# A build-time scheduler that reserves the shared SBUF port of VectorE and GpSimd, with new priorities, in a two-layer attention and RG-LRU block

## The chip, the cores and the metric

The kernel runs on one core of one Trainium2 chip, in one launch. The metric is the device time of that launch in microseconds (us). The engines are named as the profile names them: PE (TensorE matmul) and PEld (its weight load), DVE (VectorE), ACT (ScalarE), POOL (GpSimd), SP (SyncE, which issues most DMAs).

## What is computed

One sequence of 1024 latent tokens `x` and 256 context tokens `ctx`, width 1024, passes through two layers. Layer 0 is windowed grouped-query attention (16 heads, 4 key/value heads, 128-token blocks, all context keys in the same softmax, a sink logit per head), layer 1 is a bidirectional RG-LRU. A squared-ReLU MLP of width 4096 follows each. Only the latent stream is returned.

```python
for i in range(DEPTH):                       # DEPTH = 2
    mx = split(silu(c) @ ada_w[i] + ada_b[i], 6); mc = split(silu(c_ctx) @ ada_w[i] + ada_b[i], 6)
    h_x = modulate(rms_norm(x, g[0]), mx[0], mx[1]); h_c = modulate(rms_norm(ctx, g[0]), mc[0], mc[1])
    y_x, y_c = attention_mixer(...) if i % 2 == 0 else rglru_mixer(...)
    x = x + mx[2] * rms_norm(y_x, g[1])
    x = x + mx[5] * rms_norm(sqrelu_mlp(modulate(rms_norm(x, g[2]), mx[3], mx[4]), w1[i], w2[i]), g[3])
    # the same for ctx, in layer 0 only
...
# rglru_coeffs (d = direction), then a scan h = a * h + bx over the tokens
r = sigmoid(u @ w_a[d] + b_a[d]); i = sigmoid(u @ w_i[d] + b_i[d])
log_a = -8 * softplus(-lam[d]) * r
a, bx = exp(log_a), sqrt(-expm1(2 * log_a)) * (i * u)
...
y_x = (gelu(h_x @ w_gate) * (rec_forward + rec_backward)) @ w_out
```

## The kernel before, in words

Tokens lie in 8 latent and 2 context tiles of 128. Each fp32 operand of a matmul is split into a high part, its value rounded to fp32r by a cast (line 254, on ACT or DVE), and a low part, the value minus the high part (a tensor_tensor with two SBUF inputs, on DVE or GpSimd). A product is three matmuls: lines 259, 260 and 261. So the stream of matmuls is fed by casts on ACT or DVE and subtractions on DVE or GpSimd. Those subtractions stand in line 638 for the attention weights (`w`), line 679 for the first layer's normed inputs (`h`), lines 1658 and 1909 for later ones, line 1590 for the output projection's weights, line 2220 for its inputs `z`.

Nothing in the program text fixes the order of the work. A class `Plan` (lines 43 to 183) takes every operation with the engine or engines that may do it, a duration in ns, a priority (`key`), its dependences and its buffers (`add`, `any`). `order` then plays the plan through at build time: it starts the operation that can start earliest, among those within `eps` of it on the same engine the one of lowest key; where an operation may go to a second engine, it goes there only if it would end there no later than on the first one plus `alt`. `emit` writes each engine's instructions in that order, and on the chip each engine runs its own list in order and waits for semaphores.

There are four plans, played one after the other: `project` (keys `KEYS0`: norms, the modulation rows, weight splits, q, k and v, rope), the attention (`KEYS`), one for MLP 0 and everything up to and including layer 1's recurrence, output projection and residual (`KEYS2`), and MLP 1 (`KEYS3`). In a plan with `cal` set, the durations go through the line `CAL`. It is set in `KEYS2` alone (from the last part of MLP 0 on), and there `order` also knows of the port that DVE and GpSimd share: an operation in the set `two` (one that may go to either engine, or is marked) takes up to 0.43 of its length longer on DVE if it starts while GpSimd works on one.

The lines that the change and the prediction speak of:
- line 589 (`row`): a modulation row, DVE multiplies a 128x1024 tile of weights `raw` by the SiLU vector `srow` and sums it; 57 of them in `project`. Line 593 (`row_pool`): the same product on GpSimd, with the sum on ACT (line 596), for those context rows whose entry in the tables `cp` and `cq` is 1: 23 of 40. Line 1249: rows of the same kind later on.
- line 805: the low part of `q` (`qd`), line 572: the scaling `xn` by the norm (on GpSimd, ACT or DVE).
- layer 1's recurrence: lines 2112, 2116, 2120 and 2144 make gates and inputs of the scans, line 2152 is the scan (on a 128x1024 tile forward, two of 512 backward, 256 for context), lines 2185 and 2188 add the two directions and multiply by the gate, line 2220 splits the result.
- line 1746: `y<-y,py`, DVE adds a PSUM tile of the output projection to `y`; PE waits for it where it needs the PSUM tile again.
- lines 1690 to 1720: norm and residual between sub-layers (`part`, `root`, the product with `G` in line 1704, `x` in line 1706).

Of the kernel before, what the change touches and what calls it, by code (L numbers as in the profile page):

```python
# [42 lines left out]
class Plan:  # L43
    ENG = {"PE": mybir.EngineType.PE, "ACT": mybir.EngineType.Activation, "DVE": mybir.EngineType.DVE, "Pool": mybir.EngineType.Pool}
    CAL = {"PE": (1.045, 0), "ACT": (1, 105), "DVE": (1.077, 35), "Pool": (1.24, -56)}
    LAT = {"PE": 230, "ACT": 140, "DVE": 135, "Pool": 150, "DMA": 100, "Q": 900}

    def __init__(self, slots, keys, start={}):
        self.keys = keys
        self.start = start  # L50
# [35 lines left out]
    def order(self):  # L86
# [2192 lines left out]
```

## Time and profile before

| | |
|---|---|
| median of 3 runs | 2811.51 us (2810.71 to 2811.72) |
| the profiled execution's own time | 2807.43 us |
| its span, first to last instruction | 2805.7 us |
| granted TensorE clock, mean | 0.978 |
| PE busy | 2654.4 us, 95%, 12886 instructions |
| PEld busy | 2194.4 us, 78% |
| DVE busy | 2072.5 us, 74%, 3088 instructions |
| ACT busy | 1130.3 us, 40%, 2105 instructions |
| POOL busy | 899.1 us, 32%, 767 instructions |
| DMA | 392.23 MB, mean 140 GB/s |

How to read it: the profile is one execution. Its own time is 4.1 us under the median of the runs, and 1.7 us above its span. Busy shares are means over stages of very different make-up, so the windows view further down, which gives busy time by stretch, tells more than this table. The stretches used there are: 0 to 239 us (`project`), 239 to 660 (the rest of the projections, attention), 660 to 805 (attention's end, start of MLP 0), 805 to 1480 (MLP 0), 1480 to 1800 (its end, residual, start of layer 1), 1800 to 2080 (recurrence and output projection), 2080 to 2185 (residual, start of MLP 1), 2185 to 2780 (MLP 1).

### The profile page before, as it was taken

What the parts mean: (1) busy time and instruction counts of PE and PEld (TensorE: products, weight loads), DVE (VectorE), ACT (ScalarE), POOL (GpSimd) and SP (SyncE); (2) the same over time, 40 slices, a digit from 0 to 9 for tenths busy, and PEclk for the clock granted to TensorE, in tenths of its full rate; (3) what the DMA queues carried; (4) which work ended last, traced back from release to release, by engine and by line L of the source; (5) the groups of instructions that cost most, each with busy time, mean ns of one, the idle gap of its engine ahead of it and who ended that gap; (6) DMA issues with size and microseconds to landing.
All of it is one profiled execution on the core that took longest, in us unless ns stands there. A gap on an engine that the chain in (4) does not pass through costs nothing.

```text
span 2805.7 us, 35386 instructions
## 1 busy us (share of the span) xinstructions
PE 2654.4 (95%) x12886; PEld 2194.4 (78%) x12886; DVE 2072.5 (74%) x3088; ACT 1130.3 (40%) x2105; POOL 899.1 (32%) x767
## 2 busy tenths in 40 slices
PE   6798999998999999999999999989888999999997
PEld 4677788877788888888888888877666888888886
DVE  8988999997777776766657667699699776654546
ACT  5325777776322223211115434777535222221101
POOL 7653344444411103221116211254258211111113
PEclk9899999999999999999999999999999999999999
DMA  6462321214255556655554235654242333333323
GB/s 235 154 224 87 117 76 46 69 46 173 79 183 176 182 191 199 191 186 167 191 164 156 81 105 202 209 213 170 71 156 78 112 120 110 132 125 98 116 75 125
DMA packets 132613, 392.23 MB, mean 140 GB/s; under 512 B 14756, under 2 KB 17748, under 8 KB 128600
## 3 DMA queue, kind: packets, MB, share of 16 engines
q1 hardware_dynamic: 128984, 377.40, 39.9%
q10 hardware_dynamic: 3456, 12.58, 1.1%
q8 instruction: 101, 1.65, 0.3%
q14 instruction: 72, 0.59, 0.1%
HBM read 280.58 MB, written 109.35 MB: 139 GB/s over the span
## 4 chain that ended last, share of the span: by engine, by line
PE 68%; DVE 13%; POOL 4%; ACT 4%; issue 3%; DMA 2%; SPq 0%; DVEq 0%; ACTq 0%; POOLq 0%
PE pf L261 10%; PE pf L259 10%; PE pf L260 10%; PE py L260 9%; PE py L261 9%; PE py L259 9%; PE py L1103 2%; PE tp L1020 1%; DVE x L1706 1%; PE pv L1034 1%; DVE sc L990 1%; PE pg L260 1%; PE pg L259 1%; PE pg L261 1%; DVE gi L2152 1%
## 5 line engine op out<-in xcount | busy, mean ns | idle before, releaser
L260 PE MATMUL pf<-h,w 128*128 128x512 f32 (+1 forms) x1400 | 511.3, 365 | 5.9 <-POOL h L1658 5.6
L261 PE MATMUL pf<-h,w 128*128 128x512 f32 (+1 forms) x1400 | 511.3, 365 | 4.1 <-DVE w L1444 3.1
L259 PE MATMUL pf<-h,w 128*128 128x512 f32 (+1 forms) x1400 | 512.0, 366 | 1.6 <-ACT hf L1653 1.6
L1565 DVE TENSOR_TENSOR y<-y,py 128x512 f32<-128x512 f32 x268 | 183.0, 685 | 272.6 <-PE py L261 272.6
L260 PEld LDWEIGHTS pf<-h,w 128*128 128x128 f32 x1400 | 265.1, 189 | 48.6 <-POOL h L1658 6.8
L261 PEld LDWEIGHTS pf<-h,w 128*128 128x128 f32 x1400 | 264.8, 189 | 48.1 <-DVE w L1444 3.9
L259 PEld LDWEIGHTS pf<-h,w 128*128 128x128 f32 x1400 | 265.1, 189 | 44.7 <-ACT hf L1653 2.0
L1538 POOL TENSOR_TENSOR hw<-raw,hw 128x512 fp32r<-128x512 f32 x78 | 109.4, 1408 | 580.5 <-DVE hw L254 306.7
L254 ACT CAST w<-raw 128x1024 fp32r<-128x1024 f32 x126 | 131.9, 1049 | 320.0 <-PE pf L261 107.5
L259 PE MATMUL py<-hw,hw 128*128 128x512 f32 x592 | 230.4, 389 | 0.0
L261 PE MATMUL py<-hw,hw 128*128 128x512 f32 x592 | 230.3, 389 | 0.0
L260 PE MATMUL py<-hw,hw 128*128 128x512 f32 x592 | 230.3, 389 | 0.0
L254 ACT CAST hw<-raw 128x512 fp32r<-128x512 f32 x113 | 68.7, 621 | 387.5 <-DMA raw<-in_w 166.0
L1014 POOL TENSOR_SCALAR P<-P,sc 128x640 f32<-128x640 f32 (+2 forms) x160 | 118.3, 752 | 180.0 <-DVE sc L1011 94.3
L259 PE MATMUL py<-w,hw 128*128 128x512 f32 x432 | 168.2, 389 | 0.0
L261 PE MATMUL py<-w,hw 128*128 128x512 f32 x432 | 168.1, 389 | 0.0
L260 PE MATMUL py<-w,hw 128*128 128x512 f32 x432 | 168.1, 389 | 0.0
L1103 PE MATMUL py<-w,oT 128*128 128x512 f32 x480 | 146.5, 409 | 2.8 <-DVE w L938 2.1
L997 ACT ACTIVATE P<-S,sc 128x640 f32<-128x640 f32 (+2 forms) x160 | 113.9, 712 | 52.8 <-DVE sc L991 35.4
L259 PEld LDWEIGHTS py<-hw,hw 128*128 128x128 f32 x592 | 111.1, 188 | 23.2
L260 PEld LDWEIGHTS py<-hw,hw 128*128 128x128 f32 x592 | 111.1, 188 | 23.1
L261 PEld LDWEIGHTS py<-hw,hw 128*128 128x128 f32 x592 | 111.1, 188 | 23.0
(298 smaller groups left out, 6405.4 us busy)
## 6 DMA issues: line engine op xcount, KB each, us to landing
raw<-in_w SPq DMA_DIRECT2D x128, 512.0 KB, 3.8
raw<-in_ada_t SPq DMA_DIRECT2D x96, 512.0 KB, 4.6
raw<-hid_d SPq DMA_DIRECT2D x64, 512.0 KB, 4.5
w<-ws_d SPq DMA_DIRECT2D x30, 1024.0 KB, 6.2
hid_d<-c SPq DMA_DIRECT2D x112, 256.0 KB, 2.3
ws_d<-pw SPq DMA_DIRECT2D x80, 256.0 KB, 2.9
x<-x_d SPq DMA_DIRECT2D x26, 512.0 KB, 4.5
x_d<-x SPq DMA_DIRECT2D x24, 512.0 KB, 2.6
```

The lines of the kernel that those rows point to most:

```text
L254: (e.copy if e is self.nc.scalar else e.tensor_copy)(out=out, in_=x)
L259: mm(o, lhsT=lh, rhs=rh, start=start, stop=False, skip_group_check=on)
L260: mm(o, lhsT=lh, rhs=rl, start=False, stop=False, skip_group_check=on)
L261: mm(o, lhsT=ll, rhs=rh, start=False, stop=stop, skip_group_check=on)
L990: nc.vector.tensor_reduce(out=nmx[:, j:j + 1], in_=z["S", j][:, 256:256 + n], op=ALU.max, axis=AX.X, negate=True)
L997: nc.scalar.activation(out=z["P"][j][:, :n], in_=z["S", j][:, 256:256 + n], func=AF.Exp, scale=0.125, bias=negm[:, j:j + 1], accum_out=l[: ...
L1014: nc.gpsimd.tensor_scalar(out=z["P"][j][:, :n], in0=z["P"][j][:, :n], scalar1=z["sc"][3][:, j:j + 1], scalar2=1.0, op0=ALU.mult, op1=ALU.mult)
L1020: nc.tensor.transpose(z["tp", i][:, j * P:(j + 1) * P], z["P"][j][:, i * P:(i + 1) * P], self.ident)
L1034: mm(z["acc"], lhsT=v, rhs=z["pt", i][:, e], start=i + e == 0, stop=e == 1 and i == len(keys) - 1)
L1103: nc.tensor.matmul(z["ps", n], lhsT=oT[k // 2][2]["oT"][:, x, k % 2], rhs=Wo[k][:, w, n * 512:(n + 1) * 512], start=m == 0, stop=m == 3 * ...
L1538: e.tensor_tensor(out=z[n][:, 1], in0=z["raw"][:, s], in1=z[n][:, 0].bitcast(F32), op=ALU.subtract)
L1565: nc.vector.tensor_tensor(out=y, in0=y, in1=z["ps"], op=ALU.add)
```

## The change

The planner treats the port as something that one engine holds at a time. Each operation names the engines on which it holds the port (`two`, a string: "DVE", "Pool", "DVE Pool" or empty). `order` keeps until when each engine's last such operation lasts (`held`), and starts one on DVE no earlier than GpSimd's ends, and the other way round; the surcharge of up to 0.43 is gone. This concerns the plan alone: no semaphore and no instruction is added on the chip. `cal` is now set in `KEYS0` and `KEYS` too, so the port is modelled in three of the four plans; `KEYS3` (MLP 1) is as before. From `CAL` the factors and offsets of DVE, ACT and GpSimd go, and many durations are given anew. The keys of `KEYS0` and `KEYS2` are other numbers: `alt` goes from 1800 to -300 in `KEYS0` and from 600 to 150 in `KEYS2`; in the tables `cp` and `cq` 10 entries are 1 instead of 23.

```diff
-    CAL = {"PE": (1.045, 0), "ACT": (1, 105), "DVE": (1.077, 35), "Pool": (1.24, -56)}
+    CAL = {"PE": (1.045, 0), "DVE": (1, 0)}
...
-        self.two = set()
...
-    def add(self, eng, ns, key, fn, deps=(), take=(), free=(), tab=None, two=False):
+        self.two = {}
...
+    def add(self, eng, ns, key, fn, deps=(), take=(), free=(), tab=None, two=""):
...
-        if two or many and "Pool" in eng and "DVE" in eng:
-            self.two.add(len(self.ops))
+        self.two[len(self.ops)] = two.split() if self.cal else []
...
-        return self.add(order, [table[e] for e in order], key, fn, deps, take, free, tab)
+        return self.add(order, [table[e] for e in order], key, fn, deps, take, free, tab, table.get("two", ""))
...
-        bus = pool = 0.0
+        bus = 0.0
+        held = dict(DVE=0.0, Pool=0.0)
...
+            if e in self.two[i]:
+                t = max(t, held["Pool" if e == "DVE" else "DVE"])
...
-            if i in self.two and self.cal:
-                if eng == "Pool":
-                    pool = t + d
-                elif eng == "DVE" and pool > t:
-                    d += min(0.43 * d, 0.3 * (pool - t))
...
+            if eng in self.two[i]:
+                held[eng] = f
...
-COPY = lambda n, psum=False: {"ACT": n * 0.833 + (53 if psum else 93), "DVE": n * 1.04 + 70 if psum else n * 0.52 + 70}
-PAIR = lambda n: {"DVE": n * 1.04 + 70, "Pool": n * 2.1 + 150}
+COPY = lambda n, psum=False: {"ACT": n * 0.833 + (53 if psum else 93), "DVE": n * 1.04 + 70 if psum else n * 0.52 + 70,
+                            "two": "" if psum else "DVE"}
+PAIR = lambda n: {"DVE": n * 1.04 + 70, "Pool": n * 2.1 + 150, "two": "DVE Pool"}
...
-                    o = p.add("Pool", 2300, key, lambda s=s, ft=ft: row_pool(B[s, ft]), [o, crow[1]])
...
+                    o = p.add("Pool", 2300, key, lambda s=s, ft=ft: row_pool(B[s, ft]), [o, crow[1]], two="Pool")
...
-                    o = p.add("DVE", 1134, key, lambda s=s, ft=ft: row(B[s, ft], B[s, ft], 1, s, ft), [o, crow[1]], free=["raw0"])
...
+                    o = p.add("DVE", 1134, key, lambda s=s, ft=ft: row(B[s, ft], B[s, ft], 1, s, ft), [o, crow[1]], free=["raw0"], two="DVE")
...
-            mod[ft, 0] = p.any({"DVE": 210, "Pool": 410}, "DVE Pool", key, lambda e, ft=ft: post(e, ft, 0), lat)
...
+            mod[ft, 0] = p.any({"DVE": 290, "Pool": 850, "two": "DVE Pool"}, "DVE Pool", key, lambda e, ft=ft: post(e, ft, 0), lat)
...
-                        x = p.add("DVE", 2130, q, f_scan(0, D, 0), [x, bb[jt, 0]], free=[own["a%d" % jt]], two=True)
...
+                        x = p.add("DVE", 2262, q, f_scan(0, D, 0), [x, bb[jt, 0]], free=[own["a%d" % jt]], two="DVE")
...
-            t = p.add("DVE", n * 1.04 + 140, k + Z["v"] * d, lambda j=j: top(j), [s])
...
+            t = p.add("DVE", n * 1.04 + 260, k + Z["v"] * d, lambda j=j: top(j), [s])
...
-                 gp=4.47, c0=43.61, cp=4.66, w0=278.53, wp=17.22, r0=455.78, spill=5, tab=311.53, alt=600, ba=7, bb=8, bw=15, bg=5, bo=0, hm=1, cal=1,
...
+                 gp=0.64, c0=17.8, cp=2.79, w0=318.76, wp=49.35, r0=537.21, spill=5, tab=116.3, alt=150, ba=7, bb=19, bw=11, bg=10, bo=0, hm=1, cal=1,
```

What it does to the instructions, counted in the lists of instructions that the plans emit: GpSimd has 586 instead of 772, DVE 3112 instead of 2934, ACT 1827 instead of 1829. In `project`, line 593 on GpSimd goes from 23 to 10 and line 589 on DVE from 57 to 70; line 805 from 10 on GpSimd and 6 on DVE to 4 and 12; line 679 from 14 and 10 to 5 and 19; line 638 from 2 and 10 to 0 and 12; line 572 has 9 instead of 5 on GpSimd. In the recurrence, GpSimd goes from 64 instructions to none (lines 2112, 2120, 2185, 2188, 2220 and 1590 are all on DVE), in the residual behind it from 75 to 52. ACT's table loads go from 24 to 27. In the attention little moves (254 instead of 257 on GpSimd), and MLP 1 is as it was.

Two places in the order. The first is DVE at the start of `project`, up to its first low part `h` of line 679 (`raw` a tile of modulation weights, `junkd` a scratch tile, `mod` the sums). Before:

```order
L589 SCALAR_TENSOR_TENSOR junkd,mod<-raw_196,srow_152 128x1024
L589 SCALAR_TENSOR_TENSOR junkd,mod<-raw_206,srow_152 128x1024
L585 TENSOR_TENSOR mod<-mod,small 128x2
L586 TENSOR_SCALAR mod<-mod,small 128x1
L589 SCALAR_TENSOR_TENSOR raw_206,mod<-raw_206,srow_153 128x1024
L589 SCALAR_TENSOR_TENSOR junkd,mod<-raw_226,srow_152 128x1024
L679 TENSOR_TENSOR h_245<-hf_242,h_245 128x512
```

and with the change:

```order
L589 SCALAR_TENSOR_TENSOR junkd,mod<-raw_276,srow_152 128x1024
L589 SCALAR_TENSOR_TENSOR raw_276,mod<-raw_276,srow_153 128x1024
L589 SCALAR_TENSOR_TENSOR junkd,mod<-raw_284,srow_152 128x1024
L585 TENSOR_TENSOR mod<-mod,small 128x2
L586 TENSOR_SCALAR mod<-mod,small 128x1
L589 SCALAR_TENSOR_TENSOR raw_284,mod<-raw_284,srow_153 128x1024
L254 CAST h_326<-hf_317 128x512
L585 TENSOR_TENSOR mod<-mod,small 128x2
L586 TENSOR_SCALAR mod<-mod,small 128x1
L679 TENSOR_TENSOR h_326<-hf_312,h_326 128x512
```

Before, 4 rows of line 589 and one of line 638 stand ahead of the first `h` on DVE, now 11 and 4; the first group of tokens is now that of tiles 4 to 7, and two `h` follow each other.

The second is DVE in the last forward block of the recurrence, between two additions `y<-y,py` of line 1746 (`ga` decay, `gi` input and result of the scan, `gr` and `grc` gates of latent and context, `gac` context decay). Before:

```order
L2112 TENSOR_TENSOR gw_17655<-ga_2845_17481 128x1024
L2116 SCALAR_TENSOR_TENSOR grc_2850_17486<-gw_17646,grc_2850_17486 128x256
L2116 SCALAR_TENSOR_TENSOR gr_2843_17479<-gw_17655,gr_2843_17479 128x1024
L2116 SCALAR_TENSOR_TENSOR gr_2846_17482<-gw_17658,gr_2846_17482 128x1024
L2144 TENSOR_TENSOR grc_2849_17485<-grc_2849_17485 128x256
L2144 TENSOR_TENSOR gi_2844_17480<-gi_2844_17480,gr_2843_17479 128x1024
L2144 TENSOR_TENSOR grc_2850_17486<-grc_2850_17486 128x256
L2144 TENSOR_TENSOR gi_2847_17483<-gi_2847_17483,gr_2846_17482 128x1024
L2152 SCALAR_TENSOR_TENSOR grc_2849_17485<-gac_17487,grc_2849_17485 128x256
L2152 SCALAR_TENSOR_TENSOR grc_2850_17486<-gac_17487,grc_2850_17486 128x256
L2152 SCALAR_TENSOR_TENSOR gi_2844_17480<-ga_2845_17481,grc_2849_17485,gi_2844_17480 128x1024
L2152 SCALAR_TENSOR_TENSOR gi_2847_17483<-ga_2848_17484,grc_2850_17486,gi_2847_17483 128x1024
L1746 TENSOR_TENSOR y_17336<-y_17336,py_17636 128x512
```

and with the change:

```order
L1746 TENSOR_TENSOR y_17299<-y_17299,py_17575 128x512
L2144 TENSOR_TENSOR grc_2843_17435<-grc_2843_17435 128x256
L1746 TENSOR_TENSOR y_17299<-y_17299,py_17588 128x512
L2144 TENSOR_TENSOR gi_2838_17430<-gi_2838_17430,gr_2837_17429 128x1024
L2144 TENSOR_TENSOR grc_2844_17436<-grc_2844_17436 128x256
L2144 TENSOR_TENSOR gi_2841_17433<-gi_2841_17433,gr_2840_17432 128x1024
L2152 SCALAR_TENSOR_TENSOR grc_2843_17435<-gac_17437,grc_2843_17435 128x256
L2152 SCALAR_TENSOR_TENSOR grc_2844_17436<-gac_17437,grc_2844_17436 128x256
L2152 SCALAR_TENSOR_TENSOR gi_2838_17430<-ga_2839_17431,grc_2843_17435,gi_2838_17430 128x1024
L2152 SCALAR_TENSOR_TENSOR gi_2841_17433<-ga_2842_17434,grc_2844_17436,gi_2841_17433 128x1024
L1746 TENSOR_TENSOR y_17309<-y_17309,py_17599 128x512
```

Twelve rows stood between two additions to `y`, from line 2112 to the last scan; now an addition stands among the products of line 2144, and 7 rows are left between the last two.

## Rows read from the trace of the kernel before

**Rows 1.** Windows: stretch, length, busy (xcount) PE, PEld, DVE, ACT, POOL, clock, DMA share, GB/s

```profile
0.00:239.00 239.00, 188.74 (x761) 143.60 (x761) 205.06 (x298) 91.35 (x146) 149.11 (x89) 0.92 0.55 195
239.00:660.00 421.00, 405.82 (x2494) 330.87 (x2493) 384.31 (x928) 318.55 (x803) 182.50 (x252) 1.00 0.22 70
660.00:805.00 145.00, 130.21 (x661) 109.11 (x660) 106.66 (x116) 59.70 (x103) 60.44 (x45) 0.95 0.44 153
805.00:1480.00 675.00, 675.00 (x3259) 570.02 (x3258) 459.65 (x657) 154.27 (x252) 111.34 (x90) 1.00 0.56 182
1480.00:1800.00 320.00, 315.01 (x1578) 266.75 (x1577) 212.25 (x261) 156.56 (x260) 90.98 (x79) 1.00 0.42 148
1800.00:2080.00 280.00, 243.00 (x1064) 197.89 (x1063) 241.23 (x233) 175.65 (x248) 116.40 (x62) 0.91 0.45 159
2080.00:2185.00 105.00, 93.11 (x420) 76.69 (x419) 99.71 (x106) 56.94 (x113) 86.13 (x71) 0.93 0.25 91
2185.00:2780.00 595.00, 595.00 (x2626) 492.68 (x2625) 342.15 (x469) 110.84 (x164) 87.53 (x63) 1.00 0.34 111
```

**Rows 2.** Lines by form, DVE, whole run: xcount | busy us, mean ns | idle before

```profile
L1249 DVE SCALAR_TENSOR_TENSOR junk<-raw,srow 128x1024 bf16<-128x1024 f32 x56 | 68.9, 1231 | 8.2 <-DMA raw<-in_ada_t 8.2
...
L589 DVE SCALAR_TENSOR_TENSOR junk<-raw,srow 128x1024 bf16<-128x1024 f32 x24 | 44.9, 1870 | 4.9 <-DMA raw<-in_ada_t 4.5
...
L589 DVE SCALAR_TENSOR_TENSOR junkd<-raw,srow 128x1024 bf16<-128x1024 f32 x16 | 29.1, 1821 | 0.2
...
L589 DVE SCALAR_TENSOR_TENSOR raw<-raw,srow 128x1024 f32<-128x1024 f32 x17 | 25.1, 1484 | 1.2 <-ACT srow L254 0.9
...
L638 DVE TENSOR_TENSOR w<-raw,w 128x1024 fp32r<-128x1024 f32 x10 | 20.0, 1998 | 3.5 <-ACT w L254 3.5
...
L805 DVE TENSOR_TENSOR qd<-t,t 128x1024 f32<-128x1024 f32 x6 | 15.7, 2613 | 0.2
```

**Rows 3.** Lines by form, GpSimd, whole run

```profile
L593 POOL TENSOR_TENSOR raw<-raw,srow 128x1024 f32<-128x1024 f32 x23 | 63.9, 2785 | 27.2 <-DVE junk L589 15.7 <-issue 4.6 <-DVE mod L783 3.8
...
L805 POOL TENSOR_TENSOR qd<-t,t 128x1024 f32<-128x1024 f32 x10 | 28.9, 2895 | 19.6 <-DVE t L821 9.7 <-DMA q_d<-qd 5.2 <-issue 2.5
```

**Rows 4.** One line each: duration ns min/median/max, first and last start

```profile
L2188 DVE TENSOR_TENSOR ge<-ge,gi x12: 678/1434/2830, 1836.1 to 2052.7; 128x512 f32<-128x512 f32 x12
...
L1746 DVE TENSOR_TENSOR y<-y,py x84: 656/677/689, 1489.9 to 2107.3; 128x512 f32<-128x512 f32 x84
```

**Rows 5.** Waits of PE, 0 to 239 us: total us, times, longest

```profile
PE pq L261 <- DVE h L679: 11.9, 5, 6.1
```

**Rows 6.** One line: line 679 on DVE

```profile
L679 DVE TENSOR_TENSOR h<-hf,h x10: 424/688/1749, 21.3 to 92.6; 128x512 fp32r<-128x512 f32 x9, 128x256 fp32r<-128x256 f32 x1
```

**Rows 7.** Waits of PE, 1800 to 2080 us

```profile
PE py L259 <- DVE y L1746: 22.7, 4, 12.4
```

**Rows 8.** Timeline of DVE: start us, us, instruction xcount [idle before]

```profile
1984.92 0.69 DVE L1746 TENSOR_TENSOR y<-y,py 128x512 f32<-128x512 f32 x1 [0.34 <-PE py L261]
...
1998.35 6.48 DVE L2152 TENSOR_TENSOR_SCAN gi<-ga,grc,gi 128x1024 f32<-128x1024 f32 x2
2004.76 4.36 DVE L1746 TENSOR_TENSOR y<-y,py 128x512 f32<-128x512 f32 x7
...
2038.80 1.27 DVE L2152 TENSOR_TENSOR_SCAN grc<-gac,grc 128x256 f32<-128x256 f32 x2
2039.98 2.44 DVE L2152 TENSOR_TENSOR_SCAN gi<-ga,grc,gi 128x512 f32<-128x512 f32 x2
```

**Rows 9.** Timeline of PE, the wait of that stretch

```profile
2005.47 0.79 PE L259 MATMUL py<-w,z 128*128 128x512 f32 x1 [12.43 <-DVE y L1746]
```

**Rows 10.** Lines by form, DVE, 2080 to 2185 us

```profile
L1706 DVE SCALAR_TENSOR_TENSOR x<-y,ss,x 128x512 f32<-128x512 f32 x16 | 18.9, 1196 | 1.4 <-POOL ss L1698 0.8 <-POOL y L1704 0.6
...
L1893 DVE TENSOR_TENSOR hf<-hf,hf 128x512 f32<-128x512 f32 x9 | 12.2, 1383 | 0.0
```

**Rows 11.** One line: line 991, beside GpSimd in the attention

```profile
L991 DVE SCALAR_TENSOR_TENSOR sc<-sc,nsink x160: 158/160/1070, 240.9 to 651.0; 128x1 f32<-128x1 f32 x160
```

More of the change, by code (lines that the diff above doesn't have):

```diff
@@ L533, in project @@
         o = p.add("ACT", 950, -99, sig, [o], take=["raw0"], tab="sigmoid")
-        o = p.add("DVE", 1134, -99, mul, [o], free=["raw0"])
+        o = p.add("DVE", 1134, -99, mul, [o], free=["raw0"], two="DVE")
         k = p.add("DVE", 230, -99, pick, take=["hf"])
@@ L576, in project @@
             o = p.add("Pool", 750, key, root, [o])
-            xop[t] = p.any({"Pool": 1095, "ACT": 950, "DVE": 602}, "Pool ACT DVE", key, scale, [o])
+            xop[t] = p.any({"Pool": 1095, "ACT": 950, "DVE": 602, "two": "DVE"}, "Pool ACT DVE", key, scale, [o])
         mod, ada = {}, []
@@ L608, in project @@
                 o = p.add("Q", LOAD, key, load, take=["raw0"])
-                o = p.add("DVE", 1134, key, latent, [o, crow[0]])
+                o = p.add("DVE", 1134, key, latent, [o, crow[0]], two="DVE")
                 lat.append(o)
@@ L720, in project @@
         o = p.add("Q", 400, 30, mask, [swr], take=["t"])
-        p.add("DVE", 280, 30, mask_copy, [o], free=["t"])
+        p.add("DVE", 280, 30, mask_copy, [o], free=["t"], two="DVE")
         ps, pop = {}, {}
@@ L911, in plan_kv @@
         k = p.add("DVE", 335, key(13), lambda: nc.vector.tensor_tensor(
-            out=z["khl"][:, :, 1], in0=z["k3"], in1=z["khl"][:, :, 0].bitcast(F32), op=ALU.subtract), [k])
+            out=z["khl"][:, :, 1], in0=z["k3"], in1=z["khl"][:, :, 0].bitcast(F32), op=ALU.subtract), [k], two="DVE")
         def put():
@@ L1085, in plan_unit @@
         k = at("tp", 5 * Z["dt"] + Z["o"])
-        o = p.add("ACT", 530, k, out_a, [last], take=["oo"])
-        o = p.add("DVE", 670, k, out_b, [o], free=["pv"])
+        o = p.add("ACT", 560, k, out_a, [last], take=["oo"])
+        o = p.add("DVE", 680, k, out_b, [o], free=["pv"])
         o = p.add("ACT", 305, k, out_hi, [o], take=["oT"])
-        lo_ = p.add("Pool", 690, k, out_lo, [o], free=["oo"])
+        lo_ = p.add("Pool", 690, k, out_lo, [o], free=["oo"], two="Pool")
         return o, lo_, z
@@ L1698, in root @@
                 nc.gpsimd.tensor_tensor(out=q[:, 2:3], in0=q[:, 2:3], in1=self.mhalf, op=ALU.pow)
-            sq = [p.add(("ACT", "DVE"), (615, 605), key, lambda e, n=n: part(e, n), [deps[n]]) for n in range(2)]
+            sq = [p.add(("ACT", "DVE"), (615, 605), key, lambda e, n=n: part(e, n), [deps[n]], two="DVE") for n in range(2)]
             return sq, p.add("Pool", 830, key, root, sq)
@@ L1706, in plan_residual @@
             o.append(p.add("DVE", 665, key, lambda n=n: nc.vector.scalar_tensor_tensor(
-                out=x(n), in0=y(n), scalar=z["a"][:, 2:3], in1=x(n), op0=ALU.mult, op1=ALU.add), [r, g[n], xop], two=True))
+                out=x(n), in0=y(n), scalar=z["a"][:, 2:3], in1=x(n), op0=ALU.mult, op1=ALU.add), [r, g[n], xop], two="DVE"))
         z["g"] = g
@@ L1721, in plan_residual @@
             sq, r = stat("b", x, o)
-            z["op"] = p.any({"ACT": 1040, "Pool": 1100, "DVE": 665}, "ACT DVE Pool", key, scale, [r])
+            z["op"] = p.any({"ACT": 1040, "Pool": 1100, "DVE": 665, "two": "DVE"}, "ACT DVE Pool", key, scale, [r])
         return z
```

48 lines of the change are left out of this document (24 added, 24 removed).

## The prediction

> **What bounds the kernel now.** I read the windows view first, because the shares over the whole run (PE 95%) mean little for a change that moves work between DVE and GpSimd. In each stretch the reader is to compare PE's busy time with the stretch's length [rows 1]. From 805 to 1480 and from 2185 to 2780 PE is busy for all of it (675.00 of 675.00, 595.00 of 595.00): nothing that DVE or GpSimd do there can move the end, as long as they keep up. PE's idle time lies elsewhere: 239.00 - 188.74 = 50.3 us in the first stretch, 15.2 from 239 to 660, 14.8 from 660 to 805, 5.0 from 1480 to 1800, 37.0 from 1800 to 2080, 11.9 from 2080 to 2185. That is 134 us, and it caps the gain. In the first and in the two last of these DVE is the fullest engine beside PE (205 of 239, 241 of 280, 99.7 of 105), and GpSimd has its heaviest use (149, 116 and 86). There PE waits for what DVE delivers: 11.9 us for line 679 [rows 5] and 22.7 us for line 1746 [rows 7].
>
> Next, what DVE's time consists of. A multiplication of two 128x1024 tiles in SBUF takes 1231 ns in line 1249, late in the run and in the mean of 56, which I take as undisturbed; the same operation in line 589 takes 1870, 1821 and 1484 ns in the stretch in which GpSimd runs line 593 and the products of line 805, 2785 and 2895 ns each [rows 2, 3]. Line 2188 varies between 678 and 2830 ns for one shape, while line 1746, which has one operand in PSUM, never leaves 656 to 689 ns [rows 4]. So what stretches DVE is a second operand in SBUF beside a working GpSimd. That is what the changed plan keeps apart, in time and by giving GpSimd less.
>
> **The change, part by part.** The sum is made against the profiled execution's own 2807.43 us; the median of the runs, 2811.51, lies 4.1 us above, and I add that at the end.
>
> *A, start of the run (0 to 239 us).* What DVE loses there to GpSimd, by the rows that show it [rows 2]: line 589, 99.1 us for 57 instructions, less 57 x 1.231 = 70.2, is 28.9; line 638, 10 x (1.998 - 1.231) = 7.7; line 805, 6 x (2.613 - 1.231) = 8.3; together 45 us. What is added to DVE: 13 rows of line 589, 6 of line 805 and 2 of line 638, 21 x 1.231 = 25.9, and 9 halves of `h` at 0.688 [rows 6], of which two are 256 wide or less, about 5; some casts go to ACT, 3 less: +28. Line 593 still goes to GpSimd 10 times of 23. If contention went entirely, DVE would win 45 - 28 = 17 us; if it stayed in proportion (10/23 of 45 = 20 us), it would lose 3. The changed plan starts neither engine's port work during the other's, so by its own rule nothing is lost, but its clock drifts from the chip's: DMA arrivals, PE's start. I take the middle, nearer to the upper value: **10 us**. DVE also idles 34 us of the stretch, and PE 50; a better order of starting could give more, so the upper end is 27 (17 plus 10 of that idle time), the lower -3. Line 2188's worst case, 2830 ns against 678, shows that one meeting costs up to 2.15 us [rows 4]; the mean here was 45 / 33 = 1.36 for each large GpSimd operation. The Trainium skill ("SBUF — State Buffer", Who interferes with whom) says that whichever engine starts first holds the shared ports for its whole instruction and the other is blocked. By that rule A would be 17 if no pair ever met, and -22 if each of the 14 remaining operations cost DVE its whole 2.785 us; line 2188's spread agrees with it. What ACT loses (13 sums of line 596) is on an engine that is busy 91 of 239 us; its cover is wide. The DMAs are issued by SP in another order (the first tokens loaded are tile 4's), the same number of bytes.
>
> *B, 660 to 805 us.* 14.8 us of idle PE at the start of MLP 0, when DVE is busy 107 and GpSimd 60. GpSimd gives part of its splits to DVE. **4 us**, ends -2 and 10.
>
> *C, recurrence and output projection (1800 to 2080).* GpSimd's work goes to DVE altogether. The longest stall of PE is 12.43 us, for line 1746 [rows 9]. DVE's list shows it: an addition to `y` ends at 1985.61, and the next starts at 2004.76, 19.15 us later; in between lie twelve gate and scan instructions, with two context scans and two scans stretched to 6.48 us by GpSimd [rows 8]. In the new order 7 instructions lie between the last two additions: `gi` twice (2 x 1.231, a product of that size, rows 2), `grc` (0.41, a third of it), two context scans (1.27 for two, undisturbed) and two forward scans, each as long as the two backward halves, 2.44 undisturbed [rows 8]. That is 2.46 + 0.41 + 1.27 + 4.88 = 9.0 us, 10.1 less than 19.15, and so about 10 of the 12.43 us of stall. Of the remaining 10.3 us of such waits [rows 7] I take half, 5, since DVE's scans and products are no longer stretched; of the other idle time (37.0 - 22.7 = 14.3) 2 us. **17 us.** Against it: DVE takes over 64 instructions. Line 2188 shows what each costs alone: 0.678 us for 512 columns [rows 4]; 64 times that, 43 us, is about what DVE has idle here (280 - 241 = 39) plus what it stops losing. So the lower end is 0, the upper all 37.0.
>
> *D, residual and start of MLP 1 (2080 to 2185).* DVE is full (99.7 of 105), with line 1706 at 1196 ns and line 1893 at 1383 ns [rows 10] where 512 columns alone take 0.678. GpSimd loses 23 instructions, DVE gains 23: 16 us added, against (1.196 - 0.678) x 16 + (1.383 - 0.678) x 9 = 14.6 saved in these two lines alone, more in others. **5 us** of the 11.9, ends 0 and 11.9.
>
> *E, attention (239 to 660).* Nearly the same instructions in another order, with longer durations in the plan. **1 us**, ends -5 and 6. ACT's three additional table loads fall in C, where ACT is busy 176 of 280; I cost them at nothing, the cover being that idle time.
>
> Sum: 10 + 4 + 17 + 5 + 1 = 37 us. 2807.4 - 37 = 2770.4 in a profiled execution, **2774** as a median.
>
> **The rivals.** The measurement can tell about 0.2%, 5.6 us, from no change: faster is below 2805.9, slower above 2817.1.
>
> *Slow start.* In the new list 11 rows of line 589 and 4 of line 638 come before the first `h` on DVE, before the change 4 and 1: 10 x 1.231 = 12.3 us more. The first `h` stood at 21.3 us [rows 6], and PE's products wait for it. For it: DVE is the fullest engine there. Against: two `h` now follow each other, and no product needed them all. If A thus gives -10 instead of 10, the sum is 17 and the time 2794.
>
> *Unreserved ports.* The plan marks no port for a one-input GpSimd scaling such as line 572, which goes from 5 to 9 there. Line 991, tiny, runs beside one-input GpSimd work in the attention: median 160 ns, up to 1070 [rows 11]. Nine times 0.9 us, 8 us, off A: time 2782. The Trainium skill ("SBUF — State Buffer", Who interferes with whom) says a DVE instruction with two SBUF inputs contends with any GpSimd instruction that reads SBUF; by that rule this would apply, and the trace agrees in that maximum, though the median shows that it is rare.
>
> *Stalls close further.* A 27, C 25, D 8 as the idle time allows: 60 us, time 2751. For it: idle PE time in these stretches is 99 us. Against: other waits take their place.
>
> *Slower: the reservation exists only in the plan.* On the chip nothing stops a DVE instruction from starting during one of GpSimd. 14 large GpSimd operations remain (10 of line 593, 4 of line 805) of 33. Before, 45 us were lost on 33, 1.36 us each. If each now costs DVE its whole 2.785 us [rows 3], 39 us stay lost, only 6 are saved, and 28 are added: DVE and PE end 22 us later there. If C and the rest give 12 in that case (the long stall alone), the time is 2811.5 + 10 = 2821. It decides where more than 17 us remain lost, that is over 1.2 us for each remaining operation. For it: the plan's clock cannot be exact over 239 us with DMAs in it. Against: 1.36 was the mean without any plan for it.
>
> **How the numbers follow.** Forecast 0.50 (its own range 2754 to 2794, from A between 0 and 20 and C between 7 and 27 with the others fixed), slow start 0.12, unreserved ports 0.08, stalls close further 0.12, the reservation fails 0.18; of the last 0.08 ends within the band, since C may give more than 12, and 0.10 above it. So faster 0.82, same 0.08, slower 0.10. The range reaches from below the fourth case, 2746, to the edge of the band, 2806; left out is the failing reservation and the end of the fourth.
>
> **What would show it.** Right: line 589 near 1.25 us in the mean; PE idle 0 to 239 us down by about 10; no wait of PE for line 1746 over 4 us; PE still without idle time in MLP 0 and MLP 1; forward scans at about 2.4 us. Wrong: line 589 still above 1.6 us; a new wait of PE for line 679 or 638 in the first 60 us; DVE at 100% in the recurrence with PE waiting for line 2220 or 2116; or PE idle for weights in the output projection.

## The result, and the profile after

The change makes the kernel faster: 2770.49 us in the median of 4 runs (2767.64 to 2771.97) against 2811.61 for the kernel before in 4 runs beside it; the ratio is 0.9852, 95% interval 0.9839 to 0.9866. Forecast were 2774 us and a range of 2746 to 2806. The profiled execution has a span of 2767.4 us, 38.3 less than before.

The page of the kernel after, busy time by engine:

```profile
span 2767.4 us, 35278 instructions
...
PE 2634.8 (95%) x12886; PEld 2187.4 (79%) x12886; DVE 2018.8 (73%) x3281; ACT 1122.3 (41%) x2088; POOL 596.5 (22%) x581
```

GpSimd works a third less, and DVE, which took that work over, is busy 53.7 us less, not more. PE too is busy 19.6 us less with the same 12886 matmuls. So only 18.7 of the 38.3 us are idle time of PE that went; the larger half is PE's busy time.

To see where the 38.3 us went, stretches of equal time don't help, since the two kernels are at other work at one time. So I cut both at the same work, at starts of PE's lines in the trace. The view of single lines of the kernel after (duration ns min/median/max, first and last start):

```profile
L880 PE MATMUL pq<-w,h x240: 387/390/775, 178.6 to 270.0; 128*128 128x512 f32 x120
...
L1644 PE MATMUL ph<-ident,xn x80: 270/273/477, 659.5 to 715.6; 128*128 128x128 f32 x80
...
L343 PE MATMUL gt<-ident,mod x6: 270/271/421, 155.0 to 1445.1; 128*8 128x128 f32 x6
...
L261 PE MATMUL pg<-uhc,w x80: 278/283/283, 1603.6 to 1989.3; 128*128 128x256 f32 x80
...
L1644 PE MATMUL ph<-ident,y x144: 270/273/476, 1492.9 to 2115.8; 128*128 128x128 f32 x144
```

The cuts are the first matmul of line 880 (end of `project`'s own products), the first of line 1644 (MLP 0), the last of line 343 (residual and recurrence), the last gate product `pg` of the context (rest of the output projection, residual) and the last of line 1644 (MLP 1, to the end). Stage lengths in us, read in the same way for every kernel of this study. Each row is one profiled execution; that of noheld lies 4.8 us under the median of its runs, that of before 4.2, so a few us in one stage prove little by themselves:

| kernel | project | attention | MLP 0 | recurrence | residual | MLP 1 | span |
|---|---|---|---|---|---|---|---|
| before | 189.8 | 481.3 | 789.9 | 561.2 | 128.1 | 655.4 | 2805.7 |
| after | 178.6 | 480.9 | 785.6 | 544.2 | 126.5 | 651.6 | 2767.4 |
| noheld | 190.6 | 482.3 | 787.5 | 556.8 | 128.4 | 657.8 | 2803.4 |
| newkeys_oldplan | 188.9 | 479.3 | 788.7 | 566.1 | 128.2 | 658.0 | 2809.2 |
| oldkeys | 187.5 | 480.6 | 788.4 | 544.6 | 133.6 | 653.9 | 2788.6 |
| before_dveonly | 178.1 | 482.8 | 789.9 | 553.9 | 125.5 | 653.5 | 2783.7 |
| dveonly | 184.6 | 486.2 | 787.2 | 540.6 | 120.1 | 651.1 | 2769.8 |
| dveonly_held | 189.5 | 481.4 | 784.9 | 540.0 | 120.7 | 651.2 | 2767.7 |
| rows23 | 186.6 | 485.7 | 784.8 | 545.4 | 126.6 | 651.6 | 2780.7 |
| rows0 | 173.3 | 481.0 | 785.0 | 544.9 | 126.4 | 651.5 | 2762.1 |
| xnheld | 172.5 | 483.8 | 785.1 | 541.5 | 124.5 | 656.3 | 2763.7 |
| x5early | 174.4 | 481.0 | 784.3 | 545.1 | 126.6 | 651.5 | 2762.9 |
| combo | 168.1 | 486.0 | 784.6 | 538.8 | 121.6 | 651.2 | 2750.3 |
| combo_x5 | 168.6 | 479.3 | 785.6 | 536.6 | 121.2 | 651.2 | 2742.5 |

From before to after: project 11.2, attention 0.4, MLP 0 4.3, recurrence 17.0, residual 1.6, MLP 1 3.8; together 38.3. Of MLP 0's 4.3 us, 2.5 are idle time of PE (14.7 to 12.2), of MLP 1's 3.8 us 2.3.

*Project.* The windows view up to the end of the same 571 matmuls, before, with two pieces of it:

```profile
0.00:190.00 190.00, 145.81 (x571) 108.78 (x572) 164.48 (x238) 73.53 (x112) 128.57 (x81) 0.92 0.55 199
20.00:50.00 30.00, 19.26 (x69) 13.12 (x68) 24.94 (x36) 14.26 (x22) 27.00 (x25) 0.88 0.53 196
50.00:80.00 30.00, 18.01 (x77) 13.39 (x75) 27.33 (x25) 13.22 (x21) 25.95 (x16) 0.84 0.51 176
```

and after:

```profile
0.00:178.80 178.80, 134.26 (x571) 104.24 (x572) 151.36 (x272) 62.40 (x96) 67.99 (x48) 0.97 0.58 207
20.00:50.00 30.00, 5.54 (x20) 3.99 (x21) 20.98 (x40) 10.39 (x16) 20.11 (x15) 1.00 0.76 283
50.00:80.00 30.00, 28.05 (x135) 22.50 (x135) 29.65 (x57) 14.75 (x24) 12.52 (x7) 0.94 0.23 71
```

PE's idle time is the same, 190.0 - 145.8 = 44.2 and 178.8 - 134.3 = 44.5 us. The 11 us are in PE's busy time, and a good part of that is PE's clock. Before, PE's first product came at 19.5 us, and from 20 to 80 us PE was broken off time and again, at 0.88 and 0.84; after, it waits once and then runs on, but for a few short breaks. The clock column (the last but two) says too much for both kernels: it counts the first 25.5 us before and the first 47.4 us after, of which the trace has no clock record, as 1.00, though the products there are as long as at 0.50. PE's timeline before shows the turn:

```profile
24.34 0.63 PE L260 MATMUL pq<-w,h 128*128 128x512 f32 x1
24.77 0.63 PE L261 MATMUL pq<-w,h 128*128 128x512 f32 x1
...
26.03 0.39 PE L260 MATMUL pq<-w,h 128*128 128x512 f32 x1
26.26 0.40 PE L261 MATMUL pq<-w,h 128*128 128x512 f32 x1
```

One product starts 0.43 us behind the other in the first pair and 0.23 us in the second. With that first time and the stretches at 0.50 taken together, PE was busy at the low level for 36 us before and for 19 after. At these two distances the 17 us of difference are worth about 8 us, an estimate; the other 3 to 4 us of busy time were not taken apart. PE's waits in the view of waits, 0 to 190 us, are now:

```profile
PE ph L665 <- POOL xn L572: 26.4, 2, 24.4
PE sp L545 <- DVE sg L526: 11.7, 1, 11.7
PE gt L343 <- DVE mod L335: 5.7, 1, 5.7
PE pq L261 <- DVE h L679: 0.5, 1, 0.5
```

The 11.9 us for line 679 [rows 5] are 0.5 now, and 24.4 us stand in one piece before the first product (46.8 us instead of 19.5). DVE's and GpSimd's lines that answer to [rows 2, 3]:

```profile
L589 DVE SCALAR_TENSOR_TENSOR raw<-raw,srow 128x1024 f32<-128x1024 f32 x30 | 36.0, 1218 | 0.3
L589 DVE SCALAR_TENSOR_TENSOR junk<-raw,srow 128x1024 bf16<-128x1024 f32 x24 | 33.2, 1383 | 5.3 <-DMA raw<-in_ada_t 5.2
...
L589 DVE SCALAR_TENSOR_TENSOR junkd<-raw,srow 128x1024 bf16<-128x1024 f32 x16 | 22.7, 1417 | 1.3 <-ACT srow L254 1.2
L805 DVE TENSOR_TENSOR qd<-t,t 128x1024 f32<-128x1024 f32 x12 | 20.4, 1715 | 2.3 <-DMA q_d<-qd 2.2
...
L638 DVE TENSOR_TENSOR w<-raw,w 128x1024 fp32r<-128x1024 f32 x12 | 14.6, 1218 | 5.8 <-ACT w L254 5.8
```

```profile
L593 POOL TENSOR_TENSOR raw<-raw,srow 128x1024 f32<-128x1024 f32 x10 | 27.7, 2772 | 70.3 <-DMA raw<-in_ada_t 35.0 <-DVE junk L589 32.9 <-issue 2.5
L572 POOL TENSOR_SCALAR xn<-xn,rs 128x1024 f32<-128x1024 f32 x9 | 18.9, 2105 | 0.9
```

All 70 rows of line 589 take 91.9 us, 1313 ns in the mean, where 57 took 99.1. Not all contention is gone: line 805 is at 1715 ns.

*Recurrence.* The same 2536 matmuls, before and after:

```profile
1461.00:2022.20 561.20, 529.52 (x2536) 442.60 (x2535) 418.44 (x457) 315.65 (x485) 189.22 (x131) 0.97 0.43 152
...
1445.10:1989.30 544.20, 523.29 (x2536) 440.30 (x2535) 396.88 (x540) 319.16 (x482) 49.75 (x54) 0.98 0.45 156
```

Idle time falls from 31.7 to 20.9, busy time by 6.2. The longest waits of PE in these two stretches, before and then after:

```profile
PE py L259 <- DVE y L1746: 12.4, 1, 12.4
PE py L260 <- DVE w L1590: 4.9, 3, 2.3
PE pg L259 <- DMA w<-ws_d: 4.1, 1, 4.1
PE pg L260 <- DVE uh L2025: 4.0, 3, 1.7
```

```profile
PE py L259 <- DVE y L1746: 9.0, 1, 9.0
...
PE py L259 <- ACT y L1744: 3.0, 2, 2.7
PE pg L260 <- DVE uh L2025: 1.0, 1, 1.0
```

The waits that went are those for the weight splits of line 1590, for a load and for line 2025; the one for line 1746, on which the prediction rested, is only 3.4 us shorter, and waits of 3.1 and 3.0 us for lines 1720 and 1744 came anew. DVE, then GpSimd, then PE at that place in the timeline of the kernel after:

```profile
1955.33 0.68 DVE L1746 TENSOR_TENSOR y<-y,py 128x512 f32<-128x512 f32 x1
...
1958.53 2.29 DVE L2152 TENSOR_TENSOR_SCAN grc<-gac,grc 128x256 f32<-128x256 f32 x2
1960.74 6.48 DVE L2152 TENSOR_TENSOR_SCAN gi<-ga,grc,gi 128x1024 f32<-128x1024 f32 x2
1967.15 4.36 DVE L1746 TENSOR_TENSOR y<-y,py 128x512 f32<-128x512 f32 x7
...
1957.65 10.64 POOL L2220 TENSOR_TENSOR z<-zb,z 128x512 fp32r<-128x512 f32 x4 [405.70 <-ACT z L254]
...
1967.86 0.80 PE L259 MATMUL py<-w,z 128*128 128x512 f32 x1 [9.05 <-DVE y L1746]
1968.45 0.63 PE L260 MATMUL py<-w,z 128*128 128x512 f32 x1
```

The two scans take 6.48 us exactly as in [rows 8], while four splits of line 2220 run on GpSimd, after 405.70 us of idling, though the plan had reserved the port. PE's wait is 9.05 us; it was 12.43 [rows 9].

A second such wait ends 51 us later, in the last block of the recurrence, which the cuts put into the stage "residual". There two splits of line 1590 run on GpSimd beside the scans, and a pair of scans that took 2.44 us in [rows 8] takes 4.46. PE's wait, GpSimd and DVE:

```profile
PE py L259 <- DVE y L1746: 12.9, 1, 12.9
...
2005.17 5.95 POOL L1590 TENSOR_TENSOR w<-raw,w 128x1024 fp32r<-128x1024 f32 x2 [36.88 <-ACT w L254]
...
2008.91 4.46 DVE L2152 TENSOR_TENSOR_SCAN gi<-ga,grc,gi 128x512 f32<-128x512 f32 x2
```

The two waits make 21.9 us; before, the four of [rows 7] made 22.7. The sentence ahead of the prediction that GpSimd has no instruction left in the recurrence, lines 2220 and 1590 included, was wrong: six splits of line 2220 and two of line 1590 run on it, from 1957.7 us on.

### The profile page after: what moved, and what is told of

It is laid out like the page before. It is cut to its first block, busy times and chain, and to the rows that moved or that the text cites. A ratio compares the mean times of both kernels' runs of the same rounds, so it can differ in the third digit from the quotient of the medians.

```text
span 2767.4 us, 35278 instructions
## 1 busy us (share of the span) xinstructions
PE 2634.8 (95%) x12886; PEld 2187.4 (79%) x12886; DVE 2018.8 (73%) x3281; ACT 1122.3 (41%) x2088; POOL 596.5 (22%) x581
## 5 line engine op out<-in xcount | busy, mean ns | idle before, releaser
L260 PEld LDWEIGHTS pf<-h,w 128*128 128x128 f32 x1400 | 264.6, 189 | 47.4 <-DVE h L1658 6.1
L1538 POOL TENSOR_TENSOR hw<-raw,hw 128x512 fp32r<-128x512 f32 x49 | 69.2, 1416 | 563.2 <-DVE hw L254 433.4
L261 PE MATMUL py<-w,hw 128*128 128x512 f32 x432 | 168.1, 389 | 0.0
L260 PE MATMUL py<-w,hw 128*128 128x512 f32 x432 | 168.1, 389 | 0.0
L1538 DVE TENSOR_TENSOR hw<-raw,hw 128x512 fp32r<-128x512 f32 x153 | 113.8, 765 | 25.0 <-ACT hw L254 23.0
L259 PEld LDWEIGHTS py<-hw,hw 128*128 128x128 f32 x592 | 111.1, 188 | 23.3
L261 PEld LDWEIGHTS py<-hw,hw 128*128 128x128 f32 x592 | 111.1, 188 | 23.1
```

Of the source, the lines that this page charges most:

```text
L259: mm(o, lhsT=lh, rhs=rh, start=start, stop=False, skip_group_check=on)
L260: mm(o, lhsT=lh, rhs=rl, start=False, stop=False, skip_group_check=on)
L261: mm(o, lhsT=ll, rhs=rh, start=False, stop=stop, skip_group_check=on)
L1538: e.tensor_tensor(out=z[n][:, 1], in0=z["raw"][:, s], in1=z[n][:, 0].bitcast(F32), op=ALU.subtract)
```

## The experiments

Two theories stood at the start. **P**: the gain is time that DVE no longer loses to GpSimd. **K**: it is the order that the new numbers make. Later **Q** came out of P: what helps is that GpSimd gets less two-input work, not that the plan keeps the engines apart in time. Ratios are to the kernel before, run on the same chip in the same set; in brackets the 95% interval. The kernel after stands at 0.9852.

**The reservation off, the numbers kept** (noheld):

```diff
-            if e in self.two[i]:
+            if e in self.two[i] and False:
```

> The kernel after the change, with its keys and durations, but the planner no longer lets an instruction wait for the other engine's hold on the port (the check in `first` is switched off). GpSimd then gets 679 instructions instead of 586 (line 2185 twelve times, 2112 eleven, 805 eight). Theory P (the port: the gain is time that DVE no longer loses to GpSimd): most of the 41 us comes back, project ends about 8 us later, the recurrence about 12, the residual about 4: 2795 us and more, and DVE's forward scans go from 2.5 back towards 3 us. Theory K (the keys: the gain is the order that the new numbers make, above all a late but unbroken start of PE and the earlier gate products): under 2780 us.

Measured: 2810.02 us, ratio 1.0001 [0.9992, 1.0011]. The whole gain is gone: 12.0 us of it in project, 12.6 in the recurrence. The lines of DVE and GpSimd by form (line 2185 fifteen times on GpSimd, not twelve):

```profile
L589 DVE SCALAR_TENSOR_TENSOR raw<-raw,srow 128x1024 f32<-128x1024 f32 x30 | 42.8, 1434 | 0.5
...
L2152 DVE TENSOR_TENSOR_SCAN gi<-ga,gi 128x512 f32<-128x512 f32 x10 | 22.0, 2225 | 0.1
```

```profile
L2185 POOL TENSOR_TENSOR gi<-gi,gi 128x512 f32<-128x512 f32 x15 | 28.7, 1924 | 53.9 <-DVE gi L2152 42.9 <-DMA ge<-ge_d 10.9
```

The same scan has 1267 ns after the change, where line 2185 is on DVE: in the recurrence GpSimd plainly stretches DVE again. K alone falls. In project the rows say less. Those into `raw` have 1434 ns instead of 1218, but the other 40 are about as long as after the change, and all 70 take 99.3 us instead of 91.9. PE's first product comes at 45.4 us here too, and its 571 matmuls take 135.4 us, about as after the change; what is lost is idle time, 55.4 us instead of 44.5.

**The converse: the new numbers in the old planner** (newkeys_oldplan: the kernel before with `KEYS0` and `KEYS2` of after).

> The kernel before, with its planner, durations and surcharge, and the new numbers of KEYS0 and KEYS2 (no cal in KEYS0, as before). Theory P: 2795 us or more, because GpSimd works beside DVE (699 instructions on it, line 2185 eleven times). Theory K: under 2780 us. If neither, the numbers were fitted to the planner they came with and fit no other, and the time may even be above 2811.

Measured: 2811.11 us, 1.0004 [0.9995, 1.0014]. The new numbers alone are worth nothing. Project takes 10.3 us longer than after the change, though the 70 rows of line 589 are nearly as short (1356 ns in the mean, after 1313) and DVE is busy there for 150.1 us (after 151.2).

**The old numbers in the new planner** (oldkeys: after with `KEYS0` and `KEYS2` of before, `cal` set).

> The kernel after the change, planner and durations included, but with the numbers of KEYS0 and KEYS2 of the kernel before (cal set in KEYS0 as after the change; 23 rows on GpSimd, alt 1800 and 600). Theory P: most of the gain stays, 2775 to 2785 us, since the planner keeps the two engines apart by itself. Theory K: most of it goes, 2800 us and more.

Measured: 2791.05 us, 0.9939 [0.9921, 0.9957], between the two expectations. The planner with its durations gives 0.6%, and in the recurrence 16.6 of the 17.0 us; the other 0.9% need numbers that were chosen with it, above all in project (187.5 against 178.6) and in the residual (133.6 against 126.5).

**More rows on GpSimd** (rows23):

```diff
-'cp': [0, 0, 1, 0, 0, 0, 1, 0, 0, 0, 0, 0, 0, 0, 0, 0]
+'cp': [1, 0, 0, 0, 1, 1, 0, 1, 1, 1, 1, 1, 0, 1, 0, 0]
...
```

> The kernel after the change with the tables cp and cq of the kernel before: 23 instead of 10 rows of line 593 on GpSimd, nothing else changed. The planner still keeps the port apart. Theory P in the plan's sense (a large GpSimd operation costs DVE its whole length, 2.78 us, while DVE's own takes 1.23): 13 x (2.78 - 1.23) = 20 us more in the first stretch at most, at least 5. Theory that the number of rows on GpSimd does not matter because project is held by PE's start (46.8 us) and PE's work: within 3 us of 2770.

Measured: 2782.91 us, 0.9904 [0.989, 0.9919], inside P's 5 to 20 us: 0.5% worse than after, project 8.0 us longer and the attention 4.8. The 13 rows cost about 1 us each, even with the port reserved in the plan; line 589 into `junk` is at 1718 ns again.

**No row on GpSimd** (rows0: `cp` and `cq` all 0).

> The kernel after the change with none of line 593's rows on GpSimd (tables cp and cq all 0): ten more rows on DVE, 12.3 us of work there, ten GpSimd products of 2.77 us gone. If a row on GpSimd costs DVE as much as it saves (2.77 us of blocked port against 1.23 of own work, as 23 rows cost 12.4 us more than 10): 2770 or less, down to 2755 if the 13 rows' price of 0.95 us each goes on to zero rows. If the ten fit into times in which DVE has nothing to do: 2773 to 2782 us.

Measured: 2763.53 us, 0.9836 [0.9821, 0.9851], inside the first expectation. The interval overlaps that of after, so the whole run doesn't settle it; the stages do point one way, project is 5.3 us shorter and nothing else moves by 1 us.

**No two-input work on GpSimd where it is optional, without and with the reservation** (dveonly; dveonly_held has the first edit alone):

```diff
-            opts = [(e, n * self.CAL[e][0] + self.CAL[e][1] if e in self.CAL else n) for e, n in opts]
+            opts = [(e, n * self.CAL[e][0] + self.CAL[e][1] if e in self.CAL else n) for e, n in opts if not (many and two == "DVE Pool" and e == "Pool" and "ctx" not in self.keys)]
...
-            if e in self.two[i]:
+            if e in self.two[i] and False:
```

> As noheld (no reservation in the planner), but in the first and third plan every operation that could go to either DVE or GpSimd and has two SBUF inputs may go to DVE alone; the 10 rows of line 593 stay on GpSimd, unreserved. GpSimd 549 instructions, DVE 3060. Theory Q (the reservation acts only by keeping two-input work off GpSimd; the keeping apart in time is worth nothing): 2768 to 2775 us. Theory P (keeping apart in time counts): the recurrence is as good as after the change, since GpSimd has none of its instructions in both, 547 us between the last matmul before the gates' stage and the last gate product; the loss against 2770 is in project, 4 to 8 us, where ten rows of line 593 now meet DVE at random: 2775 to 2780 us.

> The kernel after the change with the reservation, and with the same restriction as dveonly: in the first and third plan the two-input operations may go to DVE alone; 551 instructions on GpSimd instead of 586 (lines 679, 805, 2220: none). If GpSimd's remaining share still helps: 2772 to 2778 us. If it only costs: 2765 to 2769 us.

Measured: 2772.83 us, 0.9872 [0.9856, 0.9889], and 2770.70 us, 0.9864 [0.9849, 0.9879]. Q's time is met; dveonly_held lies between its two ranges. The stages say where Q holds. In recurrence and residual both kernels take 660.7 us together, 10 less than after (670.7) and 24.5 less than noheld (685.2): with nothing optional left on GpSimd the reservation does nothing, and its absence costs nothing. Up to MLP 0 both need 670.8 and 670.9 us, 11 more than after: there GpSimd's nine operations of lines 679 and 805 seem to have been a help. In dveonly_held PE waits 10.6 us at one place of project for line 679, now on DVE alone; whether that comes of the engine or of the order around it is not shown. P's 4 to 8 us for unreserved rows of line 593 did not show, since the reserved kernel is no better.

**The same restriction in the kernel before** (before_dveonly).

> The kernel before, with its own planner, durations and numbers, but in the first and third plan every two-input operation that could go to either engine may go to DVE alone; the 23 rows of line 593 stay on GpSimd. Theory Q (what helps is less two-input work on GpSimd, whatever the planner knows): about as oldkeys, 2785 to 2795 us, nearly all of it from the recurrence (564 us before, about 545). If the new durations and numbers are needed for it: 2800 us and more.

Measured: 2786.82 us, 0.9925 [0.9908, 0.9941]: as much as the new planner gives with the old numbers. The time was met, the place was not: 7.3 us come from the recurrence and 11.7 from project, where the same edit did harm with the new numbers. In project DVE is even busier than before (165.5 us in 178.1, against 164.3 in 189.8). So what project takes depends by some 10 us on which order the greedy planner falls into, not on DVE's busy time alone, and a single kernel there proves little.

**Scalings reserved too** (xnheld):

```diff
-"DVE": 602, "two": "DVE"}
+"DVE": 602, "two": "DVE Pool"}
...
-"DVE": 665, "two": "DVE"}
+"DVE": 665, "two": "DVE Pool"}
```

> The kernel after the change, but the one-input scalings of lines 572 and 1720 are also reserved when they run on GpSimd; the planner then puts line 572 on ACT or DVE in all cases and line 1720 on GpSimd four times. The rival of unreserved ports: these scalings hold the port too, line 572 took 2.1 us on GpSimd beside DVE; keeping them out saves up to 9 x 0.9 = 8 us of DVE and GpSimd, 2762 to 2768 us. If that contention is hidden behind the loads that PE waits for (the first product starts at 46.8 us): 2768 to 2773 us.

Measured: 2764.21 us, 0.9838 [0.9824, 0.9853], inside the first expectation, but the interval again overlaps that of after. Project is 6.1 us shorter; PE's longest wait there is 16.7 us instead of 24.4.

**An earlier start of PE** (x5early: the key of tile 5's load in `KEYS0` from 34.89 to -60.0).

> The kernel after the change with one number changed: the key of token tile 5's load in KEYS0 from 34.89 to -60, so that the tile for which PE waited (24.4 us, up to the first product at 46.8 us) is loaded seven loads earlier, some 9 us at the 410 GB/s seen there. Theory S (project is held by when PE starts, since from then on it runs almost unbroken): project ends some 8 us earlier, 2760 to 2765 us. Theory D (project is held by DVE's work; a late start only gathers waits in one place): PE starts earlier, idles more and at a lower clock later, end within 3 us of 178.8: 2768 to 2774 us.

Measured: 2765.74 us, 0.9846 [0.9831, 0.986], so the whole run is not told apart from after. Its waits, 0 to 175 us:

```profile
PE pq L259 <- ACT w L254: 9.4, 1, 9.4
PE ph L665 <- POOL xn L572: 7.0, 3, 3.4
PE pq L261 <- DVE h L679: 4.3, 3, 2.6
```

The first product comes at 34.6 us, 12.2 earlier, and project ends 4.2 earlier. So neither theory holds alone: the wait for tile 5 falls from 24.4 us to 3.4 at most, and 9.4 us for a weight's cast and 4.3 for line 679 come in its place.

**What the runs pointed to, together** (combo: rows0, xnheld, and GpSimd out of the optional two-input work in the third plan alone; combo_x5: with x5early's number).

> What the runs so far point to: the kernel after the change with no row of line 593 on GpSimd, the scalings of lines 572 and 1720 reserved, and in the third plan (recurrence and residual) two-input operations on DVE alone; in project GpSimd keeps three of line 805 and five of line 679. If the gains add: project 5 to 8 us shorter than after the change (rows0 5.4, xnheld 6.1), recurrence 4 and residual 6 (as dveonly and dveonly_held): 2752 to 2758 us. If they are the same gain twice or DVE becomes the bound in project (some 156 us of its own work): 2760 to 2766 us.

> combo with the earlier load of tile 5 (the edit of x5early, which alone gave 4.8 us). If the two gains in project are of different kinds: 2742 to 2746 us. If the earlier load only moves waits now that the scalings are on ACT and DVE: 2747 to 2752 us.

Measured: 2748.80 us, 0.9785 [0.977, 0.9799], and 2747.58 us, 0.9787 [0.9771, 0.9804]. Here the intervals lie clear of after's: combo is a further 0.7% faster, 3 us better than the range for gains that add. The earlier load adds nothing that can be told. The page of combo, and the place of the scans in its timelines of DVE and PE:

```profile
PE 2636.0 (96%) x12886; PEld 2185.4 (79%) x12886; DVE 2018.7 (73%) x3324; ACT 1124.8 (41%) x2084; POOL 494.8 (18%) x532
```

```profile
1946.33 0.68 DVE L1746 TENSOR_TENSOR y<-y,py 128x512 f32<-128x512 f32 x1
...
1949.53 1.27 DVE L2152 TENSOR_TENSOR_SCAN grc<-gac,grc 128x256 f32<-128x256 f32 x2
1950.71 4.57 DVE L2152 TENSOR_TENSOR_SCAN gi<-ga,grc,gi 128x1024 f32<-128x1024 f32 x2
1955.20 4.37 DVE L1746 TENSOR_TENSOR y<-y,py 128x512 f32<-128x512 f32 x7
...
1955.92 0.79 PE L259 MATMUL py<-w,z 128*128 128x512 f32 x1 [6.10 <-DVE y L1746]
```

With line 2220 off GpSimd the scans take 4.57 us, and PE's wait at this place falls from 9.05 to 6.10; the second one falls from 12.9 to 8.7.

## Why the prediction was right, and which of its steps failed

That the reservation in the plan makes the gain is shown: with it off, the same kernel stands where before stood. For the recurrence and the residual the runs show what costs: two-input work on GpSimd stretches DVE's scans there, and forbidding it gives more than the reservation does. For project the way from the reservation to the time is not shown.

The sizes by stage came out close: A 10 foreseen, 11.2 measured; B 4 and 4.3; C 17 and 17.0; E 1 and 0.4; D 5, against 1.6 in the residual and 3.8 behind it. But the stages are not cut where the terms are (C runs past the end of "recurrence"), and all terms were counted in idle time of PE, of which I wrote that it "caps the gain". Idle time gave 18.7 of the 38.3 us, in project nothing and in MLP 0 2.5; PE's busy time, which no term contained, gave 19.6. That the sum agrees so well is in part luck.

Three steps inside were wrong.

*A, the way.* I took DVE's saving for an equal cut of PE's idle time, "PE idle 0 to 239 us down by about 10". PE's idle time up to the end of project did not fall, 44.2 to 44.5 us; the gain is in PE's busy time, mostly by its clock, which the term did not contain. DVE's busy time up to there fell by 13.1 us (164.5 to 151.4), near the 17 of the contention's end, but it doesn't set the length of project: in newkeys_oldplan DVE is busy for less and project takes 188.9 us, in before_dveonly for more and project takes 178.1. The rival of the slow start was right that the first `h` comes late (first product 27 us later), but not because of the rows ahead of it on DVE: PE waits for `xn` of line 572, whose tile is loaded late. And it costs less than the rival gave it, since what follows runs almost unbroken: x5early takes 12.2 us off the start and project becomes 4.2 shorter.

*C, the long stall.* "9.0 us, 10.1 less than 19.15, and so about 10 of the 12.43 us": the scans were not undisturbed, because the splits of line 2220 that stay on GpSimd were overlooked. From the end of one addition to `y` to the start of the next there are 11.1 us now, 8.0 less than 19.15, yet only 3.4 us of the stall went. The difference does not carry over one to one: before, PE ran on for 7.4 us after the last addition and then stopped; now it stops after 2.8. In combo, where the scans do run undisturbed, it is 2.8 too, and the wait is 6.10 us, not 2.3.

*C, the other waits.* Of the remaining waits for line 1746 "I take half, 5": nothing of them went, as the second wait of 12.9 us shows (the sign "no wait of PE for line 1746 over 4 us" failed twice), and all waits for line 1746 together fell by 0.8 us where 15 were foreseen. That C was still 17 comes from what the term gave 2 us or nothing: waits for splits of line 1590, for a load and for line 2025 (10.8 us of idle time went in all) and 6.2 us of busy time. That the size agrees is luck.

*The rival of a reservation that the chip doesn't keep* named a true weakness with the wrong consequence. It isn't kept (the scans of line 2152, line 805 at 1715 ns), but it also moved work off GpSimd, and in recurrence and residual that is enough to account for its use: forbidding the work gives 24.5 us against noheld, the reservation 14.5. The Trainium skill ("SBUF — State Buffer", Who interferes with whom) says that a DVE instruction with two SBUF inputs contends with a GpSimd instruction that reads SBUF, over a shared pair of ports that is an exclusive lock. The trace agrees both ways: the scan of 1267 ns takes 2225 ns beside line 2185, and four splits take 10.64 us beside the scans, where the fastest of the six takes 1.30. Those scans take 1.27 and 4.57 us in combo, and four splits at 1.30 make 5.2: together 11.0 us, an estimate, about the 10.64 us in which both were done.

```profile
L2220 POOL TENSOR_TENSOR z<-zb,z x6: 1297/2132/3251, 1957.7 to 2036.2; 128x512 fp32r<-128x512 f32 x6
```

*Unreserved ports* (forecast as a loss of 8 us): line 572 takes 2105 ns in the mean on GpSimd (1122 at the fastest), and reserving it shortens project by 6.1 us in one profile; the intervals don't separate it.

Open: whether the 5 to 6 us of rows0, xnheld and x5early in project each have the cause named or come from another order of a greedy planner, as before_dveonly against dveonly warns; by which way the reservation shortens project, since neither the length of DVE's rows nor its busy time does it alone; what `cal` in the attention's plan does by itself (0.4 us of difference there) was not tried; and the busy time of PE that went outside project was not taken apart.

## What to carry to other kernels

Where DVE is near the bound, two-input work given to GpSimd beside it makes both slower; try first to give GpSimd none, stage by stage, before teaching a planner to interleave the two, because the times in a plan made at build time are not the chip's. Forbidding it was worth more than the reservation in recurrence and residual; in project it lost 11 us with the new numbers and gained 12 with the old. Compare stages cut at the same work, not at the same time, and look at PE's busy time as well as its idle time: the same matmuls took 8.6% longer (145.8 us against 134.3) where idle time was scattered among them. And numbers fitted to one planner may be worth nothing in another: here they were worth 0.9% with it and nothing without.

## What the runs showed of the hardware that I had not expected

Equal idle time, unequal cost. TensorE's clock has two levels, 1.2 and 2.4 GHz. In project PE was busy at the lower one for 36 us before and for 19 after, with the same 571 matmuls and the same 44 us of idle time: scattered over 20 to 80 us before, mostly in one piece ahead of the first product after. PE's busy time differs by 11.6 us, about 8 of them by the clock. In the recurrence a wait of 9.05 us is followed by matmuls of 0.63 us, where 0.39 is the usual, so each long stall costs more than itself.
